# Two blocks of a diffusion transformer in one kernel: tiles moved by 128 and 96 bytes, and pieces of the modulation rows loaded one or two chunks earlier

## The chip, the core and the metric

The kernel runs on one core of one Trainium2 chip. The metric is the device time of one execution in microseconds (us); smaller is better. The profile adds a trace of one execution: every instruction's start and duration on each engine (PE is TensorE, DVE is VectorE, ACT is ScalarE, POOL is GpSimd, SP is SyncE, which issues the DMAs).

## The reference, cut to what matters

Two "macaron" transformer blocks follow each other on 256 tokens of width 1024, each with two layers, all in float32. A layer is feed-forward, mixer, feed-forward; that makes twelve phases. Each phase is preceded by a norm whose scale and shift, and followed by a residual whose gate, come from a modulation row:

```
mod = (silu(c) @ ada_w[l] + ada_b[l])            # 9 rows of 1024 for a layer
pre(h, j) = rmsnorm(h, norm_g[l, j]) * (1 + mod[:, j, 1]) + mod[:, j, 0]
x = x + 0.5 * (1 + mod[:, 0, 2]) * swiglu(pre(x, 0), ffn_wi[l, 0], ffn_wo[l, 0])
x = x + (1 + mod[:, 1, 2]) * mixer(pre(x, 1))
x = x + 0.5 * (1 + mod[:, 2, 2]) * swiglu(pre(x, 2), ffn_wi[l, 1], ffn_wo[l, 1])

swiglu(h, wi, wo): gt, up = split(h @ wi); (silu(gt) * up) @ wo      # wi 1024 x 5632, wo 2816 x 1024
```

The mixers are an HGRN2 recurrence ("hgrn") and a differential attention ("diff") in the first block, and twice a sparse attention beside a spatial gate ("nsa") in the second, whose modulation and residual differ slightly in form. All weights, some 530 MB, are read once from memory.

## The kernel before, in words

**Weights.** They come in chunks of 512 rows by 512 columns. `load_chunk` takes a chunk in two halves; each half is one DMA into a tile `raw` and is then split in two: ACT rounds it to the short float32 form (`hi`, L197), and DVE takes the rest (`lo`, L198). The pool `split` holds eight `hi` and eight `lo` tiles, four chunks in all; loading runs ahead of use as far as these go.

**Matmuls.** A product of float32 numbers is made of three matmuls on split operands. In the token-major form (`mm3`, L454 to L456) the activations are the stationary operand, which TensorE loads before the matmul (128 columns, LDWEIGHTS), and 512 columns of the weights stream past it: hi by hi, lo by hi, hi by lo. The activations are `hT` (the normed input, transposed, for the first product of a phase), `aT` (the gated hidden values of a feed-forward, for its second product), and for the mixers' last products `y`, `k`, `q`, `oT`. In the feature-major form (`feature_block`, L550 and L552) the weights are the stationary operand and the activations stream: one matmul of `hi` with 512 columns (both parts of `hT` for 256 tokens) and one of `lo` with 256 columns. Most of the first product of a feed-forward is feature-major: chunks 4 to 21 of its 34 (8 to 21 in the first phase), two chunks to a block, 70 blocks of 32 such pairs in the whole kernel. The mixer hgrn has its own feature-major form with three matmuls of 256 columns (L611 to L613).

**Modulation rows.** Each row of 1024 values is made of four pieces. A piece (`ada`) loads two tiles `araw` of 128 rows of `ada_w`; DVE multiplies each by a column of silu(c) and adds it up (`accumulate`, L264). When the eighth is in, `row_sum` adds over the partitions with TensorE: ACT and DVE split one half of the accumulator (`acch` L276, `accl` L277, one buffer each), TensorE sums it with a matrix of ones (L281, L282), and the result becomes shift, scale or gate; then the second half goes the same way.

**The order of the work.** `build` writes one queue with all chunks and, between them, the pieces for the gate of this phase and the scale and shift of the next. `ADA_SPAN` says for each kind of phase how many chunks at its start (skip) and at its end (tail) get no piece; the pieces are spread evenly over the chunks between. Loads are issued by SyncE in the queue's order; the number of pieces loaded sets when the sums of DVE and TensorE's row sums stand in their engines' orders. Every engine works through its instructions in order.

**Where tiles lie.** Pools are laid one behind another in each partition's memory: const, keep (with `hT`), raw, split (`hi`, then `lo`), tmp (with `acch`, `accl`), and then one pool per phase ("act" with `aT`, or the mixer's).

Of the kernel before, what the change touches and what calls it, by code (L numbers as in the profile page):

```python
# [10 lines left out]
F32R = mybir.dt.float32r  # L11
# [7 lines left out]
P = 128  # L19
D = 1024  # L20
# [11 lines left out]
W_LATER = 15  # L32
FFN_TR, QK_TR, HN_TR, MRG_TR, NSA_TR = 2, 1, 3, 2, 2
W5, XS, SG, RING, GF = 4, 4, 2, 5, 5
WARM = 60

ADA_SPAN = {"first": (11, 6), "ffn": (5, 5), "hgrn": (2, 11), "diff": (3, 6), "nsa": (2, 6), "last": (3, 10)}

NSA_PLAN = [(1, "setup"), (2, "spatial_load"), (6, "pick"), (6, "load_w1", 0, 0), (7, "load_w1", 1, 0),
            (8, "load_w1", 0, 1), (8, "load_w1", 1, 1), (10, "hidden", 0), (12, "hidden", 1), (15, "hidden_tr"), (16, "compressed"),  # L40
# [24 lines left out]
class Chunk:  # L65


    def __init__(self, src, nk, heads=0):
        self.src = src
        self.nk = nk  # L70
        self.heads = heads
        self.parts = None

    def hi(self, k):
        return self.parts[k // 2][0][:, k % 2, :]
# [5 lines left out]
class Net:  # L81
    def __init__(self, ctx, tc, A):
        self.tc = tc
        self.nc = tc.nc
        self.A = A
        self.const = ctx.enter_context(tc.tile_pool(name="const", bufs=1))
        self.keep = ctx.enter_context(tc.tile_pool(name="keep", bufs=1))
        self.rawp = ctx.enter_context(tc.tile_pool(name="raw", bufs=RAWS))
        self.split = ctx.enter_context(tc.tile_pool(name="split", bufs=HALVES))
        self.tmp = ctx.enter_context(tc.tile_pool(name="tmp", bufs=2))  # L90
        self.psm = ctx.enter_context(tc.tile_pool(name="psm", bufs=6, space=PSUM))
        self.pst = ctx.enter_context(tc.tile_pool(name="pst", bufs=2, space=PSUM))
        self.queue = []
        self.next_item = 0
        self.chunks = []
        self.used = [0, 0]
        self.loaded = 0
        self.pend = []
        self.row_stages = []
        self.araws = []  # L100
        self.gates = {}
        self.phase = None
        self.now = 0
        self.setup()
# [75 lines left out]
    def load_chunk(self, it):  # L180
        nc = self.nc
        it.parts = []
        for h in range((it.nk + 1) // 2):
            n = min(2, it.nk - 2 * h)
            w = it.src[-1][1]
            raw = self.raw()
            for c0, c1, src in it.src:
                if it.heads:
                    for g in range(2):
                        r0 = g * 256 + h * P  # L190
                        nc.sync.dma_start(raw[g * 64:(g + 1) * 64], src[r0:r0 + P].rearrange("(i d) n -> d i n", d=64))
                else:
                    nc.sync.dma_start(raw[:, :n, c0:c1], src[h * 256:h * 256 + n * P].rearrange("(k p) n -> p k n", p=P))
            hi = self.split.tile([P, 2, 512], F32R, tag="hi", name="hi")
            lo = self.split.tile([P, 2, 512], F32R, tag="lo", name="lo")
            r = raw[:, :n, :w]
            nc.scalar.activation(hi[:, :n, :w], r, AF.Copy)  # L197
            nc.vector.tensor_sub(lo[:, :n, :w], r, hi[:, :n, :w].bitcast(F32))  # L198
            it.parts.append((hi, lo))
# [110 lines left out]
    def warm(self):  # L310

        ps = self.bank()
        with self.later(1000):
            for _ in range(WARM):
                self.nc.tensor.matmul(ps.rearrange("p (a b) -> p a b", a=4), lhsT=self.ones,
# [1098 lines left out]
def phases(A, which=None):  # L1414
    out = []
    for b in range(2):
        s = "_2" if b else ""
        wi, wo = (A["ffn_wi"], A["ffn_wo"]) if b == 0 else (A["ffn_w_in_2"], A["ffn_w_out_2"])
        for l in range(2):
            out.append((b, l, 0, ("ffn", wi[l, 0], wo[l, 0])))  # L1420
            out.append((b, l, 1, (("hgrn", "diff")[l] if b == 0 else "nsa", l)))
            out.append((b, l, 2, ("ffn", wi[l, 1], wo[l, 1])))
    return out if which is None else [out[i] for i in which]


def build(ctx, tc, A, which=None):
    net = Net(ctx, tc, A)
    nc = tc.nc
    ph = phases(A, which)
    starts = []  # L1430
    net.next_phase = ph[0][:3]

    def diff_prep():
        net.diff_prep(A["b_qk_g"][0], A["b_lam"][0], A["b_subln"][0], 0.8 - 0.6 * math.exp(-0.3))

    def second_half():
        for kind in (1, 0):
            net.ada_first(kind, 1)
        for T in range(2):
            net.scaled(T, 1)  # L1440
            net.pre(T, (1,))
    for i, (b, l, j, spec) in enumerate(ph):
        ada = net.ada_pieces(b, l, j, 2)
        if i + 1 < len(ph):
            b2, l2, j2, _ = ph[i + 1]
            ada += net.ada_pieces(b2, l2, j2, 1) + net.ada_pieces(b2, l2, j2, 0)
        if spec[0] == "ffn":
            cs = net.ffn_chunks(spec[1], spec[2], i == 0)
        elif spec[0] == "hgrn":
            cs = net.hgrn_chunks(A["a_w_in"][0], A["a_w_out"][0])  # L1450
        elif spec[0] == "diff":
            cs = net.diff_chunks(A["b_w_in"][0], A["b_w_out"][0])
        else:
            cs = net.nsa_chunks(A["mix_w_in_2"][l], A["proj_a_2"][l], A["proj_b_2"][l], A["w_out_2"][l])
        starts.append(len(net.chunks))
        done = 0
        for n, spec_ in enumerate(cs):
            if i == 0 and n == 3:
                net.queue.append(("f", second_half))
            if i + 1 < len(ph) and ph[i + 1][3][0] == "diff" and n == len(cs) // 2:  # L1460
                net.queue.append(("f", diff_prep))
            net.add_w(*spec_)
            skip, tail = ADA_SPAN["first" if i == 0 else spec[0] if i + 1 < len(ph) else "last"]
            want = max(0, n + 1 - skip) * len(ada) // (len(cs) - skip - tail)
            while done < min(want, len(ada)):
                net.add_ada(ada[done])
                done += 1
    net.warm()
    net.ada_first(1, 0)
    for T in range(2):  # L1470
        nc.sync.dma_start(net.x[:, T, :], A["x"][0, T * P:(T + 1) * P, :])
        for h in range(2):
            net.norm_half(T, h)
    net.ada_first(0, 0)
    for T in range(2):
        net.scaled(T, 0)
        net.pre(T, (0,))
    net.ahead()
    net.condition("c_2")
    for i, (b, l, j, spec) in enumerate(ph):  # L1480
        last = i + 1 == len(ph)
        net.phase = b, l, j
        net.next_phase = None if last else ph[i + 1][:3]

        def after(T):
            if not last:
                net.pre(T)
            else:
                for h in range(2):
                    o, rstd = net.xs.pop((T, h)), net.ss[T][:, 3:4]  # L1490
                    if h == 0:
                        nc.scalar.activation(o, o, AF.Copy, scale=rstd)
                    else:
                        nc.vector.tensor_scalar(o, o, rstd, None, op0=OP.mult)
                    nc.sync.dma_start(A["out"][0, T * P:(T + 1) * P, h * 512:(h + 1) * 512], o)
        if last:
            nc.sync.dma_start(net.S, A["final_g_2"][None, :].to_broadcast([P, D]))
            net.rows[1] = None
        if spec[0] == "ffn":
            net.ffn(starts[i], after, i == 0)  # L1500
        elif spec[0] == "hgrn":
            net.hgrn(starts[i], A["a_onorm"][0], after)
        elif spec[0] == "diff":
            net.diff(starts[i], after)
        else:
            net.nsa(starts[i], l, after)
# [22 lines left out]
```

## Time and profile before

| | us |
|---|---|
| median of 3 runs | 2231.85 (2231.0 to 2233.54) |
| the profiled execution's own time | 2231.27 |
| its span, first to last instruction | 2229.5 |
| TensorE (matmuls) busy | 2188.1 (98%) |
| VectorE busy | 1787.6 (80%) |
| ScalarE busy | 1233.3 (55%) |
| mean granted TensorE clock | 0.998 |

A busy TensorE is not one at its peak: a matmul's recorded duration overlaps that of the next. What one costs in a dense stretch is read from the starts: the time from one start to the next. All durations below are of the profiled execution.

### The profile page before, as it was taken

What the parts mean: (1) busy time and instruction counts of PE and PEld (TensorE: products, weight loads), DVE (VectorE), ACT (ScalarE), POOL (GpSimd) and SP (SyncE); (2) the same over time, 40 slices, a digit from 0 to 9 for tenths busy, and PEclk for the clock granted to TensorE, in tenths of its full rate; (3) what the DMA queues carried; (4) which work ended last, traced back from release to release, by engine and by line L of the source; (5) the groups of instructions that cost most, each with busy time, mean ns of one, the idle gap of its engine ahead of it and who ended that gap; (6) DMA issues with size and microseconds to landing.
All of it is one profiled execution on the core that took longest, in us unless ns stands there. A gap on an engine that the chain in (4) does not pass through costs nothing. (4 is left out here: it accounts for less than half of the span.)

```text
span 2229.5 us, 33181 instructions
## 1 busy us (share of the span) xinstructions
PE 2188.1 (98%) x12152; PEld 1808.4 (81%) x12152; DVE 1787.6 (80%) x2481; ACT 1233.3 (55%) x2184; POOL 118.3 (5%) x164
## 2 busy tenths in 40 slices
PE   9999999999999989999999999999999999999998
PEld 6888887888888767888888787788878887777886
DVE  7888898787878789878868788887877878887664
ACT  3554645564565577564565446456446644655653
POOL 1000101000000131000000000000000001000000
PEclk9999999999999999999999999999999999999999
DMA  9888865777857766867767786676777778845553
GB/s 299 303 300 292 297 218 191 265 243 261 276 185 270 255 227 224 277 216 268 262 221 242 257 291 202 223 253 199 264 258 255 263 241 268 266 153 185 187 172 108
DMA packets 264788, 537.19 MB, mean 241 GB/s; under 512 B 22083, under 2 KB 52619, under 8 KB 264625
## 3 DMA queue, kind: packets, MB, share of 16 engines
q1 hardware_dynamic: 264184, 534.67, 72.1%
q8 instruction: 95, 1.56, 0.3%
q14 instruction: 69, 0.56, 0.1%
q10 hardware_dynamic: 440, 0.40, 0.1%
HBM read 533.95 MB, written 1.05 MB: 240 GB/s over the span
## 5 line engine op out<-in xcount | busy, mean ns | idle before, releaser
L198 DVE TENSOR_TENSOR lo<-raw,hi 128x1024 fp32r<-128x1024 f32 (+1 forms) x704 | 846.8, 1215 | 253.9 <-ACT hi L197 250.1
L197 ACT ACTIVATE hi<-raw 128x1024 fp32r<-128x1024 f32 (+1 forms) x704 | 732.7, 1055 | 524.1 <-PE mm L456 303.0
L550 PE MATMUL mm<-hT,hi 128*128 128x512 f32 x2240 | 793.6, 399 | 0.0
L552 PE MATMUL mm<-hT,lo 128*128 128x256 f32 x2240 | 629.5, 281 | 0.0
L550 PEld LDWEIGHTS mm<-hT,hi 128*128 128x128 f32 x2240 | 421.5, 188 | 103.9
L552 PEld LDWEIGHTS mm<-hT,lo 128*128 128x128 f32 x2240 | 423.8, 189 | 1.0
L454 PE MATMUL mm<-hi,hT 128*128 128x512 f32 (+1 forms) x832 | 331.0, 398 | 1.3 <-ACT hT L384 1.0
L456 PE MATMUL mm<-hi,hT 128*128 128x512 f32 (+1 forms) x832 | 324.8, 391 | 0.9 <-DVE hT L386 0.9
L455 PE MATMUL mm<-lo,hT 128*128 128x512 f32 (+1 forms) x832 | 323.3, 389 | 0.0
L456 PE MATMUL mm<-hi,aT 128*128 128x512 f32 x704 | 278.4, 395 | 0.0
L454 PE MATMUL mm<-hi,aT 128*128 128x512 f32 x704 | 278.2, 395 | 0.0
L455 PE MATMUL mm<-lo,aT 128*128 128x512 f32 x704 | 277.6, 394 | 0.0
L454 PEld LDWEIGHTS mm<-hi,hT 128*128 128x128 f32 x832 | 156.5, 188 | 40.3 <-issue 8.0
L264 DVE SCALAR_TENSOR_TENSOR acc<-araw,c_2s,acc 128x1024 f32<-128x1024 f32 x144 | 184.1, 1278 | 2.8 <-DMA araw<-ada_w 1.9
L456 PEld LDWEIGHTS mm<-hi,hT 128*128 128x128 f32 x832 | 156.5, 188 | 35.0 <-DVE hT L386 2.1
L455 PEld LDWEIGHTS mm<-lo,hT 128*128 128x128 f32 x832 | 156.6, 188 | 29.6 <-issue 0.7
L264 DVE SCALAR_TENSOR_TENSOR acc<-araw,cs,acc 128x1024 f32<-128x1024 f32 x128 | 163.5, 1278 | 10.6 <-DMA araw<-ada_w 9.9
L455 PEld LDWEIGHTS mm<-lo,aT 128*128 128x128 f32 x704 | 132.6, 188 | 30.4
L456 PEld LDWEIGHTS mm<-hi,aT 128*128 128x128 f32 x704 | 132.5, 188 | 30.4
L454 PEld LDWEIGHTS mm<-hi,aT 128*128 128x128 f32 x704 | 132.6, 188 | 30.3
L535 ACT ACTIVATE aT<-uf 128x256 fp32r<-128x256 f32 x140 | 58.2, 416 | 87.0 <-DVE uf L533 87.0
L248 POOL MEMSET acc<- 128x1024 f32 x34 | 32.5, 957 | 1240.2 <-DVE accl L277 713.2
(287 smaller groups left out, 2164.5 us busy)
## 6 DMA issues: line engine op xcount, KB each, us to landing
araw<-ada_w SPq DMA_DIRECT2D x272, 512.0 KB
raw<-ffn_wi SPq DMA_DIRECT2D x160, 512.0 KB
raw<-ffn_w_in SPq DMA_DIRECT2D x160, 512.0 KB
raw<-ffn_wo SPq DMA_DIRECT2D x88, 512.0 KB
raw<-ffn_w_out SPq DMA_DIRECT2D x88, 512.0 KB
raw<-mix_w_in SPq DMA_DIRECT2D x64, 512.0 KB
raw<-a_w_in SPq DMA_DIRECT2D x32, 512.0 KB
raw<-b_w_in SPq DMA_DIRECT2D x24, 512.0 KB
```

Source lines behind the costliest of these rows:

```text
L197: nc.scalar.activation(hi[:, :n, :w], r, AF.Copy)
L198: nc.vector.tensor_sub(lo[:, :n, :w], r, hi[:, :n, :w].bitcast(F32))
L248: nc.gpsimd.memset(st["acc"], 0.0)
L264: self.nc.vector.scalar_tensor_tensor(acc, raw, self.cs[b][:, k:k + 1], acc, op0=OP.mult, op1=OP.add)
L454: nc.tensor.matmul(ps, lhsT=h, rhs=hi, start=start and i == 0, stop=False)
L455: nc.tensor.matmul(ps, lhsT=h, rhs=lo, start=False, stop=False)
L456: nc.tensor.matmul(ps, lhsT=l, rhs=hi, start=False, stop=stop and i == c.nk - 1)
L535: nc.scalar.activation(hi, u, AF.Copy)
L550: nc.tensor.matmul(ps[f], lhsT=c.hi(k)[:, fs], rhs=x, start=kh == 0 and k == 0, stop=False, skip_group_check=True)
L552: nc.tensor.matmul(ps[f][:, 0:256], lhsT=c.lo(k)[:, fs], rhs=x[:, 0:256], start=False, stop=kh == 1 and k == 3, skip_group_check=True)
```

## The change: where tiles lie, and when pieces are loaded

First, the tiles of `split` grow from 1024 to 1088 float32 values (4352 bytes), and `hi` and `lo` are a window of 1024 values in them. For the feature-major chunks of the feed-forwards the window begins 24 values (96 bytes) into the tile, for all others at its start. Second, a tile of 32 values (128 bytes) that nobody uses is put at the head of the pool tmp; all that lies behind it, the pools of the phases too, moves by these 128 bytes. Third, in `ADA_SPAN` four kinds of phase have skip smaller and tail larger by one or two, so their pieces stand one or two chunks earlier in the queue.

Where the tiles stand in the two built programs (bytes from the start of a partition):

| tile | before | after | modulo 256, before | modulo 256, after |
|---|---|---|---|---|
| hT | 13,696 | 13,696 | 128 | 128 |
| hi, number k of 8 | 75,136 + 4096 k | 75,136 + 4352 k | 128 | 128; feature-major 224 |
| lo, number k of 8 | 107,904 + 4096 k | 109,952 + 4352 k | 128 | 128; feature-major 224 |
| acch, accl | 159,232, 161,280 | 163,456, 165,504 | 0 | 128 |
| aT, its two parts | 165,376, 187,904 | 169,600, 192,128 | 0 | 128 |
| k0, q0 (hgrn), oT0 (diff), y00 (nsa) | 173,568, 181,760, 189,952, 209,152 | 177,792, 185,984, 194,176, 213,376 | 0 | 128 |

Modulo 512 the tiles `hi` and `lo` before are all at 384; after, they are by turns at 384 and 128 (480 and 224 where shifted), `hT` stays at 384, and `aT` moves from 0 to 128. Inside a tile all operands begin at multiples of 512 bytes.

```
+FM_SHIFT = 24
-ADA_SPAN = {"first": (11, 6), "ffn": (5, 5), "hgrn": (2, 11), "diff": (3, 6), "nsa": (2, 6), "last": (3, 10)}
+ADA_SPAN = {"first": (10, 7), "ffn": (3, 7), "hgrn": (2, 11), "diff": (2, 7), "nsa": (1, 7), "last": (3, 10)}
...
+        self.feature_major = False                                 # Chunk.__init__
...
+        self.t(self.tmp, [P, 32], tag="pad", bufs=1)               # Net.__init__
...
-            hi = self.split.tile([P, 2, 512], F32R, tag="hi", name="hi")
-            lo = self.split.tile([P, 2, 512], F32R, tag="lo", name="lo")
+            s = FM_SHIFT if it.feature_major else 0
+            hi, lo = (self.split.tile([P, D + 64], F32R, tag=n, name=n)[:, s:s + D].rearrange("p (a b) -> p a b", a=2)
+                      for n in ("hi", "lo"))
...
-            net.add_w(*spec_)
+            c = net.add_w(*spec_)
+            net.chunks[c].feature_major = spec[0] == "ffn" and (8 if i == 0 else 4) <= n < 22
```

The numbers of matmuls, splits, sums and DMAs stay as they are; the new `ADA_SPAN` moves sums and row sums in the engines' orders. Lines of the kernel after are four or five higher than those before (L198 is L202, L264 is L268, L276 is L280, L277 is L281). Three places follow.

ScalarE in the first feed-forward, around the split of the second half of the first gate row (`acch`; `gate` is the first half's evacuation, `gf` and `uf` are the gated features, `hi` a weight split). Before:

```order
L197 ACTIVATE hi<-raw 128x1024
L529 ACTIVATE gf<-gf 128x256
L519 ACTIVATE gf<-mm 128x256
L291 ACTIVATE gate<-tr 128x512
L197 ACTIVATE hi<-raw 128x1024
L529 ACTIVATE gf<-gf 128x256
L276 ACTIVATE acch<-acc 128x512
```

And after:

```order
L539 ACTIVATE aT_366<-uf 128x256 x2
L201 ACTIVATE hi<-raw 128x1024 x2
L295 ACTIVATE gate<-tr 128x512
L280 ACTIVATE acch<-acc 128x512
L523 ACTIVATE gf<-mm 128x256 x2
```

The row's evacuation and split now stand ahead of the block's group of `gf`, where before they stood behind most of it.

VectorE at the same place (`lo` is the second part of a weight split, `acc<-araw` a sum of a modulation row, `accl` the second part of the row's split). Before:

```order
L264 SCALAR_TENSOR_TENSOR acc<-araw,cs,acc 128x1024
L198 TENSOR_TENSOR lo<-raw,hi 128x1024
L520 TENSOR_TENSOR gf<-gf,mm 128x256
L198 TENSOR_TENSOR lo<-raw,hi 128x1024
L520 TENSOR_TENSOR gf<-gf,mm 128x256
L264 SCALAR_TENSOR_TENSOR acc<-araw,cs,acc 128x1024
L520 TENSOR_TENSOR gf<-gf,mm 128x256
L264 SCALAR_TENSOR_TENSOR acc<-araw,cs,acc 128x1024
L520 TENSOR_TENSOR gf<-gf,mm 128x256
L198 TENSOR_TENSOR lo<-raw,hi 128x1024 x2
L277 TENSOR_TENSOR accl<-acc,acch 128x512
```

And after:

```order
L268 SCALAR_TENSOR_TENSOR acc<-araw,cs,acc 128x1024
L202 TENSOR_TENSOR lo<-raw,hi 128x1024 x2
L524 TENSOR_TENSOR gf<-gf,mm 128x256
L281 TENSOR_TENSOR accl<-acc,acch 128x512
L524 TENSOR_TENSOR gf<-gf,mm 128x256
L268 SCALAR_TENSOR_TENSOR acc<-araw,cs,acc 128x1024
```

The split of the row moved ahead of two sums, two weight splits and three `gf`; TensorE's row sum, which waits for it, moved earlier by 32 matmuls of the block.

VectorE in the mixer diff, in the first softmax (`ast` are its maxima and sums, `w<-e,ast` the finished weights, `rb`, `ra` a rotary product beside it). Before:

```order
L975 SCALAR_TENSOR_TENSOR ast<-ast,qs 128x4
L277 TENSOR_TENSOR accl<-acc,acch 128x512
L974 TENSOR_REDUCE ast<-mm 128x4
L975 SCALAR_TENSOR_TENSOR ast<-ast,qs 128x4
L979 RECIPROCAL ast<-ast 128x4
L264 SCALAR_TENSOR_TENSOR acc<-araw,cs,acc 128x1024
L979 RECIPROCAL ast<-ast 128x4
L264 SCALAR_TENSOR_TENSOR acc<-araw,cs,acc 128x1024
L981 TENSOR_SCALAR ast<-ast,lm 128x4
L198 TENSOR_TENSOR lo<-raw,hi 128x1024
L986 SCALAR_TENSOR_TENSOR w_7929<-e,ast 128x128 x4
```

And after:

```order
L979 SCALAR_TENSOR_TENSOR ast<-ast,qs 128x4
L978 TENSOR_REDUCE ast<-mm 128x4
L925 TENSOR_TENSOR w_7892<-ra,rb 128x8x16
L979 SCALAR_TENSOR_TENSOR ast<-ast,qs 128x4
L268 SCALAR_TENSOR_TENSOR acc<-araw,cs,acc 128x1024 x2
L983 RECIPROCAL ast<-ast 128x4
L268 SCALAR_TENSOR_TENSOR acc<-araw,cs,acc 128x1024 x2
L983 RECIPROCAL ast<-ast 128x4
L268 SCALAR_TENSOR_TENSOR acc<-araw,cs,acc 128x1024
L985 TENSOR_SCALAR ast<-ast,lm 128x4
L202 TENSOR_TENSOR lo<-raw,hi 128x1024
L990 SCALAR_TENSOR_TENSOR w_7943<-e,ast 128x128 x4
```

Five sums stand inside this softmax now, where two stood; they come from the later part of the phase, which has three fewer.

## Rows read from the trace of the kernel before

**Rows 1.** The page, part 1: busy us (share of the span) xinstructions.

```profile
PE 2188.1 (98%) x12152; PEld 1808.4 (81%) x12152; DVE 1787.6 (80%) x2481; ACT 1233.3 (55%) x2184; POOL 118.3 (5%) x164
```

**Rows 2.** Stretches: from:to us, length, busy us (xinstructions) of each engine, clock, DMA.

```profile
52.00:2160.00 2108.00, 2078.06 (x11714) 1726.22 (x11715) 1720.51 (x2394) 1193.88 (x2129) 108.52 (x142) 1.00 0.73 244
1097.00:1104.00 7.00, 7.00 (x33) 5.79 (x32) 6.92 (x8) 3.69 (x5) 0.00 (x0) 1.00 0.92 307
1223.00:1265.00 42.00, 42.00 (x183) 34.03 (x182) 32.18 (x32) 17.45 (x21) 0.74 (x2) 1.00 0.84 286
2070.00:2150.00 80.00, 80.00 (x455) 69.31 (x454) 55.46 (x87) 48.97 (x86) 0.00 (x0) 1.00 0.59 185
153.50:164.40 10.90, 10.90 (x64) 9.59 (x64) 10.68 (x17) 7.09 (x13) 0.00 (x0) 1.00 0.86 309
147.20:150.60 3.40, 3.26 (x10) 2.79 (x11) 2.36 (x3) 1.67 (x3) 0.96 (x1) 0.50 0.88 276
833.30:836.70 3.40, 3.40 (x13) 2.95 (x13) 3.40 (x6) 1.60 (x4) 0.00 (x0) 0.50 0.50 166
```

**Rows 3.** Timeline of PE, ends of four stretches: start us, us, instruction.

```profile
153.34 0.39 PE L550 MATMUL mm<-hT,hi 128*128 128x512 f32 x1
...
164.08 0.39 PE L550 MATMUL mm<-hT,hi 128*128 128x512 f32 x1
...
1096.67 0.39 PE L456 MATMUL mm<-hi,hT 128*128 128x512 f32 x1
...
1103.92 0.39 PE L455 MATMUL mm<-lo,hT 128*128 128x512 f32 x1
...
1222.65 0.39 PE L454 MATMUL mm<-hi,aT 128*128 128x512 f32 x1
...
1264.94 0.39 PE L456 MATMUL mm<-hi,aT 128*128 128x512 f32 x1
...
2069.86 0.40 PE L550 MATMUL mm<-hT,hi 128*128 128x512 f32 x1
...
2149.71 0.40 PE L550 MATMUL mm<-hT,hi 128*128 128x512 f32 x1
```

**Rows 4.** Groups by line: line engine op names xcount | busy us, mean ns | idle before.

```profile
L550 PE MATMUL mm<-hT,hi 128*128 128x512 f32 x2240 | 793.6, 399 | 0.0
L456 PE MATMUL mm<-hi,hT 128*128 128x512 f32 x800 | 315.3, 395 | 0.9 <-DVE hT L386 0.9
L454 PE MATMUL mm<-hi,aT 128*128 128x512 f32 x704 | 278.2, 395 | 0.0
L456 PE MATMUL mm<-hi,y 128*128 128x512 f32 x64 | 25.2, 394 | 0.0
```

**Rows 5.** Timeline of PE at the first row sum's second half; in brackets, idle before.

```profile
143.66 0.28 PE L552 MATMUL mm<-hT,lo 128*128 128x256 f32 x1
145.92 0.50 PE L281 MATMUL tr<-acch,ones 128*128 128x512 f32 x1 [1.98 <-ACT acch L276]
147.34 0.80 PE L282 MATMUL tr<-accl,ones 128*128 128x512 f32 x1 [0.93 <-DVE accl L277]
```

**Rows 6.** Timeline of ACT and DVE there.

```profile
133.27 1.99 ACT L197 ACTIVATE hi<-raw 128x1024 fp32r<-128x1024 f32 x2
136.53 1.28 DVE L264 SCALAR_TENSOR_TENSOR acc<-araw,cs,acc 128x1024 f32<-128x1024 f32 x1 [1.29 <-DMA araw<-ada_w]
144.33 2.35 DVE L198 TENSOR_TENSOR lo<-raw,hi 128x1024 fp32r<-128x1024 f32 x2
```

**Rows 7.** Waits of PE: who waited for whom, us in total, times, longest us.

```profile
PE tr L397 <- DVE xs L378: 7.5, 15, 0.8
PE tr L397 <- DVE w L921: 5.2, 3, 2.1
PE tr L397 <- DVE w L986: 1.0, 1, 1.0
```

**Rows 8.** Timeline of DVE in the mixer diff's first softmax.

```profile
804.35 0.18 DVE L979 RECIPROCAL ast<-ast 128x4 f32<-128x4 f32 x1 [1.87 <-ACT e L977]
```

## The prediction

> **What bounds the kernel.** I read the page's busy times first. TensorE is busy for 98% of the span, VectorE for 80%, ScalarE for 55% [rows 1], and the stretches say where the missing 2% lies: between 52 and 2160 us TensorE stands still for 2108.00 - 2078.06 = 30 us only [rows 2]. The rest of the span is matmul behind matmul, so the time is the number of matmuls times the distance from one start to the next, plus these 30 us. The recorded duration (395 ns) is no price, since it overlaps the next one; the reader must go to the timeline, take the first and the last start of a dense stretch, and divide by the number of matmuls between them, which the stretches give. I did it for four stretches, all at full clock (1.00):
>
> - token-major with `hT` as stationary operand: 33 matmuls of 512 columns in [rows 2], from 1096.67 to 1103.92, 7.25 us over 32 steps, 226.6 ns a step [rows 3];
> - token-major with `aT`: 183 matmuls of the same shape, from 1222.65 to 1264.94, 42.29 over 182, 232.4 ns;
> - feature-major: the 455 matmuls are 227 pairs and one more; from 2069.86 to 2149.71 are 226 pairs of 768 columns, 353.3 ns a pair;
> - feature-major again, right after a disturbance: 64 matmuls, 153.34 to 164.08, 31 pairs, 346.5 ns.
>
> The first two differ in nothing that the program says but where the operands lie. `hi`, `lo` and `hT` all stand at 128 modulo 256 bytes; `aT` stands at 0. Stationary and moving operand a multiple of 256 bytes (here even of 512) apart: the quick step. 128 bytes off that: 5.8 ns slower, every time. The last two are one instruction sequence on tiles that lie the same, and run at two steady paces; the quick one is rare, as the mean duration of L550 over all 2240 (399 ns) is that of the slow stretch and not the 0.39 of the other [rows 3, 4].
>
> **The change part by part.** *The 128 bytes before tmp.* They put `aT` at 128 modulo 256, which is where `hi` and `lo` stand unshifted. L454 to L456 with `aT` are 3 x 704 = 2112 matmuls [rows 4]. If they take the step of `hT`: 2112 x 5.8 ns = 12.2 us. After each interruption the pace has to be found again, and `hT` loses more there than `aT` does (its runs are short); I take 10 us. The `y` of nsa (3 x 64), and k, q and oT of hgrn and diff (3 x 32) move to 128 as well; their mean duration of 394 is like `aT`'s [rows 4], and 288 x 5.8 would be 1.7 us; their runs are short, so I take 1. Together 11 us, bounds 0 (the place decides nothing) and 13.9. A loss here has a case of its own below.
>
> *The 96 bytes under the feature-major weights.* Here stationary (`hi`, `lo`) and moving (`hT`) are a multiple of 512 bytes apart before, and the slow pace rules. After, they are 96 bytes off. No stretch before has 96 bytes, so I bound it. Above: if any distance costs what 128 bytes cost token-major, 5.8 ns for each of two matmuls, a pair takes 365 and 2240 pairs lose 26 us. Below: a pair at the token-major quick step by columns, 226.6 x 768 / 512 = 340 ns, gains 2240 x 13.3 = 30 us. The nearest row is the quick pace of the same instructions, 346.5: 6.8 ns a pair. One of 70 blocks and part of another have it already, so about 2180 pairs gain 14.8 us; I take 14.5, keeping both ends.
>
> *The larger split tiles* (4352 bytes) keep `hi`, `lo` at 128 modulo 256, and so should leave the 800 x 3 matmuls on `hT` [rows 4] where they are: 0, if 256 is the period (see the rivals if it is 512).
>
> *The pieces earlier.* No instruction is added; each sum (1.28 us on VectorE, [rows 6]), its two DMAs on SyncE and its row sum on TensorE move together. SyncE's weight loads between old and new place come up to two DMAs later, and VectorE's splits behind them; TensorE waits for no weight split in a long wait [rows 7], so I cost that at 0; if the cover were gone, it would be the two DMAs' sums, 2.6 us on VectorE. What can move are two known stalls.
> First feed-forward: TensorE ends at 143.66 + its step, then stands 2.0 us for `acch` and 0.9 for `accl` [rows 5], and after that its clock is at half (0.50, 1.2 GHz) for 3.4 us [rows 2], 1.7 us lost: 4.6 in all. Now `acch` is ahead of the `gf` group on ScalarE and `accl` ahead of two sums and two weight splits on VectorE, but TensorE asks 32 matmuls (5.65 us) earlier too, at about 138.1. By the old rows: ScalarE is at its two `hi` until 135.3, evacuates and splits the row by about 136.5; VectorE waits for `araw` until 136.53, sums until 137.8, splits two weights (2.35) and runs one `gf` first, so `accl` is there at about 141 [rows 6]. The wait would be 2.9 us, as before: the stall moves and stays. Value 0, bounds -4.6 and +1.5.
> Mixer diff: three more sums stand in the first softmax, 3.8 us, of which VectorE's old idle time there hides 1.87 [rows 8]; TensorE's wait for `w` L986, 1.0 us [rows 7], may become 2.9. The later rotary product, for which it waits 2.1 us [rows 7] with another 3.4 us at half clock behind it [rows 2], has three sums fewer ahead of it: -2.1 - 1.7. Value -1, bounds -3.8 and +1.9.
> The waits for `xs` (15 of up to 0.8 us, [rows 7]) hang on the last row and the norm at each phase's end; the third row's sums stay there, 0.
>
> Sum: -11 - 14.5 - 1 = -26.5 us on the execution's own 2231.3, which lies 0.6 under the median of the runs: 2205 us for the median.
>
> By the Trainium skill's page "SBUF — State Buffer" (section "Who interferes with whom") TensorE never waits on any other engine for SBUF, and only VectorE and GpSimd share ports; "TensorE: Matmul & The Clock Gate" (Part 2, step by step) adds that TensorE's two read ports are independent, so loading the next weights takes nothing from the running matmul. By that rule the place of a tile could not matter, and the sum would be that of the moved pieces alone. The steps of 226.6 and 232.4 ns speak against it, without proving that the place is what parts them.
>
> **The rivals.**
> *Near is what counts* (slower). In the trace the token-major step is best at distance 0 and worse at 128 bytes. If TensorE pays by the distance within 256 bytes, then moving the feature-major weights from 0 to 96 is a step in the wrong direction, and 2240 pairs pay up to 11.6 ns: -11 - 1 + 26 gives 2245; it decides from a pair of about 359 on, where it eats the other gains (12 / 2240 = 5.4 ns over 353.3). For it: the only two token-major distances seen. Against: feature-major runs at its slow pace at distance 0, so nearness alone does not give the quick one.
> *Feature-major keeps its pace.* Two paces on the same addresses show that what came before decides the pace, not only the place; then the 96 bytes do nothing: 2231.9 - 12 = 2220. For it: the quick stretch came right behind the half-clock stretch.
> *The period is 512 bytes, not 256.* All good stretches seen are multiples of 512. With tiles 4352 bytes apart, every second `hi` and `lo` is then 256 off `hT` and `aT`. If that costs as 128 do, half of 2400 matmuls on `hT` lose 5.8 ns (+7), `aT` and the others gain half (-5.5), feature-major half (-7): about 2225. Nothing before stands 256 apart, so neither for nor against.
> *The place does nothing.* `aT` is slower because it lies far up in the partition, or for its neighbours in time. Then only the pieces count: 2231 (2227 to 2235). It is also what the skill's rule would give. For it: no tile changes its place in this trace. Against: `y`, k, q and oT, also at 0 modulo 256, read like `aT` in phases quite unlike.
> *Feature-major goes under its quick pace*, to some 340 a pair: 2190.
>
> **How the numbers follow.** The forecast 0.48 (its own range 2197 to 2213, from the bounds of the two stalls and a restart loss of 0 to 4 us); feature-major unchanged 0.17; period 512, 0.10; nearness 0.12; no effect of place 0.08; under the quick pace 0.05. Faster or slower counts from 0.2% (4.5 us), about what a measurement here can tell. Faster is under 2227.4: the forecast, the lower pace, feature-major unchanged and the period of 512, together 0.80. Slower is over 2236.3: nearness, 0.12. Same: no effect of place, 0.08. The range goes from 2194 to 2231: it leaves out the pace of 340, nearness, and a little of the rest.
>
> **What would show it.** The four stretches, measured again: `aT` at about 227 a step (right) or 232 (the place is not it); a feature-major pair at 346 to 347, in nearly all 70 blocks, or at 353 or above 359; `hT` still at 226.6, and not every second chunk slower. In the waits, `acch` or `accl` of the first row at 2 to 3 us and a half-clock stretch behind; `w` L990 up by one or two us and the later wait for `w` gone. The prediction is wrong if the two paces do not follow the places, most of all if the feature-major pair is above 353.

## The result: 2205.8 us, 1.1% less, and the profile after

The changed kernel takes 2205.83 us (median of 4 runs, 2204.56 to 2207.33) against 2231.43 for the kernel before (4 runs beside it, 2230.53 to 2233.54): a ratio of 0.9887, 95% interval 0.9873 to 0.9900. The forecast was 2205. The span of the profiled execution falls from 2229.5 to 2202.8 us.

In the page, part 1 (busy us, share of the span, instructions), the same 12152 matmuls are busy for 28.6 us less than in [rows 1], while the other engines hardly move:

```profile
PE 2159.5 (98%) x12152; PEld 1803.0 (82%) x12152; DVE 1791.2 (81%) x2481; ACT 1232.7 (56%) x2185; POOL 117.4 (5%) x164
```

So the time went out of the matmuls themselves. To see out of which, I repeat the reading of [rows 2, 3]: stretches without any other instruction on TensorE (from:to, length, busy and instructions of PE, PEld, DVE, ACT, POOL, then clock, DMA share, GB/s), for `hT`, for `aT` and feature-major; the last row is a stretch of half clock.

```profile
1079.10:1088.60 9.50, 9.50 (x44) 7.86 (x43) 9.39 (x10) 5.34 (x6) 0.00 (x0) 1.00 0.88 293
1200.50:1240.00 39.50, 39.50 (x176) 32.72 (x175) 28.25 (x27) 15.62 (x18) 1.32 (x2) 1.00 0.81 274
2051.00:2127.00 76.00, 76.00 (x440) 66.86 (x440) 54.95 (x87) 47.36 (x83) 0.00 (x0) 1.00 0.62 189
290.10:293.50 3.40, 3.40 (x19) 3.40 (x18) 3.40 (x6) 0.22 (x1) 0.00 (x0) 0.50 0.85 263
```

The first and the last start of the three, from the timeline of PE (start us, us, instruction):

```profile
1078.77 0.39 PE L458 MATMUL mm<-hi,hT 128*128 128x512 f32 x1
...
1088.52 0.39 PE L459 MATMUL mm<-lo,hT 128*128 128x512 f32 x1
...
1200.26 0.39 PE L460 MATMUL mm<-hi,aT 128*128 128x512 f32 x1
...
1239.93 0.39 PE L458 MATMUL mm<-hi,aT 128*128 128x512 f32 x1
...
2050.82 0.39 PE L554 MATMUL mm<-hT,hi 128*128 128x512 f32 x1
...
2126.74 0.39 PE L554 MATMUL mm<-hT,hi 128*128 128x512 f32 x1
```

`hT`: 9.75 us over 43 steps, 226.7 ns, as before (226.6). `aT`: 39.67 over 175, 226.7 instead of 232.4. Feature-major: 440 matmuls are 220 pairs, 75.92 over 219, 346.7 ns instead of 353.3. The settled step of `aT` is now that of `hT`, and feature-major runs everywhere at the pace that it had before in a few short stretches alone: of the stretches of 16 pairs or more, all 36 settle (their first steps left out) at 346.6 to 346.8 ns a pair.

The groups by line (xcount | busy us, mean ns | idle before) say the same of whole kernels and are quicker to read: against [rows 4], L554 falls from 399 to 392 ns and `aT` from 395 to 390, `y` by 4, and `hT` hardly moves. They show the direction; the size must come from the starts.

```profile
L554 PE MATMUL mm<-hT,hi 128*128 128x512 f32 x2240 | 779.1, 392 | 0.0
L460 PE MATMUL mm<-hi,hT 128*128 128x512 f32 x800 | 314.6, 394 | 0.5 <-DVE hT L390 0.5
L458 PE MATMUL mm<-hi,aT 128*128 128x512 f32 x704 | 274.7, 390 | 0.0
L460 PE MATMUL mm<-hi,y 128*128 128x512 f32 x64 | 25.0, 390 | 0.0
```

Summing the steps from start to start over both whole traces gives the account of the 26.7 us of span: feature-major 794.5 to 777.5 us (-17.0, of which 2.1 is the old stall of [rows 5], which stood behind one of these matmuls, and 1.2 the pairs that then ran at half clock, so -13.7 by pace), `aT` 497.6 to 487.0 (-10.6), `y` 46.1 to 45.4 (-0.7), everything else +1.6, as the waits shifted.

The stall at the first row sum, from the timeline of PE after (in brackets idle before and its releaser):

```profile
137.73 0.39 PE L285 MATMUL tr<-acch,ones 128*128 128x512 f32 x1
139.28 0.51 PE L286 MATMUL tr<-accl,ones 128*128 128x512 f32 x1 [1.16 <-DVE accl L281]
```

In place of 1.98 and 0.93 us in [rows 5] TensorE waits 1.16 us, and no half clock follows. The waits of PE (us in total, times, longest) that answer [rows 7]:

```profile
PE tr L401 <- DVE xs L382: 8.4, 16, 0.8
...
PE tr L401 <- DVE w L925: 4.6, 3, 1.7
...
PE tr L401 <- DVE w L990: 1.2, 1, 1.2
```

The two half-clock stretches of [rows 2], at 147.2 and 833.3, are gone; one of the same length stands at 290.1, in the hgrn mixer.

### The profile page after: what moved, and what is told of

The parts are those of the page before. It is cut to its first block, busy times and chain, and to the rows that moved or that the text cites. A ratio compares the mean times of both kernels' runs of the same rounds, so it can differ in the third digit from the quotient of the medians.

```text
span 2202.8 us, 33165 instructions
## 1 busy us (share of the span) xinstructions
PE 2159.5 (98%) x12152; PEld 1803.0 (82%) x12152; DVE 1791.2 (81%) x2481; ACT 1232.7 (56%) x2185; POOL 117.4 (5%) x164
## 5 line engine op out<-in xcount | busy, mean ns | idle before, releaser
L202 DVE TENSOR_TENSOR lo<-raw,hi 128x1024 fp32r<-128x1024 f32 (+1 forms) x704 | 847.1, 1216 | 241.9 <-ACT hi L201 233.6
L554 PE MATMUL mm<-hT,hi 128*128 128x512 f32 x2240 | 779.1, 392 | 0.0
L554 PEld LDWEIGHTS mm<-hT,hi 128*128 128x128 f32 x2240 | 420.5, 188 | 92.6
L460 PE MATMUL mm<-hi,aT 128*128 128x512 f32 x704 | 274.8, 390 | 0.0
L458 PE MATMUL mm<-hi,aT 128*128 128x512 f32 x704 | 274.7, 390 | 0.0
L268 DVE SCALAR_TENSOR_TENSOR acc<-araw,c_2s,acc 128x1024 f32<-128x1024 f32 x144 | 184.5, 1281 | 1.7
L268 DVE SCALAR_TENSOR_TENSOR acc<-araw,cs,acc 128x1024 f32<-128x1024 f32 x128 | 164.0, 1282 | 12.5 <-DMA araw<-ada_w 11.6
```

Of the source, the lines that this page charges most:

```text
L268: self.nc.vector.scalar_tensor_tensor(acc, raw, self.cs[b][:, k:k + 1], acc, op0=OP.mult, op1=OP.add)
L458: nc.tensor.matmul(ps, lhsT=h, rhs=hi, start=start and i == 0, stop=False)
L460: nc.tensor.matmul(ps, lhsT=l, rhs=hi, start=False, stop=stop and i == c.nk - 1)
L554: nc.tensor.matmul(ps[f], lhsT=c.hi(k)[:, fs], rhs=x, start=kh == 0 and k == 0, stop=False, skip_group_check=True)
```

## The experiments

**One part of the change at a time.** Three kernels: the pad and the larger split tiles without a shift (`FM_SHIFT = 0`), the shift without the pad, and the pieces' places alone.

```
e1   + self.t(self.tmp, [P, 32], tag="pad", bufs=1);  tiles [P, D + 64], FM_SHIFT = 0;  ADA_SPAN of before
e2   tiles [P, D + 64], FM_SHIFT = 24, no pad;  ADA_SPAN of before
e3   the kernel before with the new ADA_SPAN
```

> The change without the 96 bytes and without the moved pieces: split tiles of 4352 bytes and the phases' tiles 128 bytes further. Place theory (TensorE's step depends on how far stationary and moving operand lie apart, modulo 256 bytes): aT's step goes from 232.4 to about 227 ns, the feature-major pair stays at 353; 2111 x 5.3 + 1 = 12 us faster, 2219 to 2220 us. Rival 'pieces' (the gain came from the sums placed earlier): no change, 2231. Rival 'both at once' (the pace of one form depends on the other's): feature-major moves as well.

> Only the 96 bytes under the feature-major weights (with the wider split tiles, a multiple of 256 for all behind them); aT stays at 0 modulo 256 and the pieces stay. Place theory: the pair goes from 353 to 346.8 ns, aT stays at 232.4; 2180 x 6.2 = 13.5 us faster, about 2218. Rival 'pieces': 2231. Rival 'nearness': slower, 2245.

> Only the pieces one or two chunks earlier; all tiles as before. Forecast of the prediction: about -1 us, 2230 (bounds 2223 to 2235). Place theory: aT's step 232.4 and the feature-major pair 353 as before. Rival 'pieces': 2210 or less.

Measured against the kernel before: tiles 2218.00 us, 0.9951 (0.9935 to 0.9966); shift 2217.78, 0.9951 (0.9938 to 0.9964); places 2228.56, 0.9994 (0.9985 to 1.0003), no difference that can be told. The product is 0.9897, against 0.9887 for the whole. The groups of the kernel with the tiles alone:

```profile
L554 PE MATMUL mm<-hT,hi 128*128 128x512 f32 x2240 | 793.2, 399 | 0.0
...
L458 PE MATMUL mm<-hi,aT 128*128 128x512 f32 x704 | 275.0, 391 | 0.0
```

and of the one with the shift alone:

```profile
L553 PE MATMUL mm<-hT,hi 128*128 128x512 f32 x2240 | 778.8, 392 | 0.0
...
L457 PE MATMUL mm<-hi,aT 128*128 128x512 f32 x704 | 278.5, 396 | 0.0
```

And the steps, from the first and last starts of one stretch each, `aT` with the tiles alone and feature-major with the shift alone:

```profile
1224.97 0.39 PE L458 MATMUL mm<-hi,aT 128*128 128x512 f32 x1
...
1254.89 0.39 PE L458 MATMUL mm<-hi,aT 128*128 128x512 f32 x1
...
2055.14 0.39 PE L553 MATMUL mm<-hT,hi 128*128 128x512 f32 x1
...
2135.22 0.39 PE L553 MATMUL mm<-hT,hi 128*128 128x512 f32 x1
```

29.92 us over 132 steps are 226.7 ns, 80.08 over 231 pairs 346.7. The other form stays slow in each: the pair at 353.3 with the tiles alone, `aT` at 232.4 (first and last phase) to 233.3 with the shift alone. Each edit moves the form that it was put under: two independent gains. Both kernels have the larger tiles, so these alone move neither.

**All tiles by 128 bytes.** If the place in the partition were what counts, moving everything would move the steps; if the distance, nothing would happen.

```
  self.const = ctx.enter_context(tc.tile_pool(name="const", bufs=1))
+ self.t(self.const, [P, 32], tag="pad", bufs=1)
```

> The kernel before with all its tiles 128 bytes further, so that hT, hi and lo stand at 0 modulo 256 and aT at 128: distances as before, places changed over. Place theory by distance: hT stays at 226.6 to 228, aT stays at 232.4, time 2231. Rival 'place by itself' (128 modulo 256 is a good place for the stationary operand, 0 a bad one): hT slows to 232, aT quickens to 227; 2360 x 4 - 2111 x 5.3 = about -2 us. Rival 'level' (aT is slow for lying far up or for its neighbours in time): both as before, and e1 shows no gain.

One run, 2231.20 us, and the groups are those of [rows 4]:

```profile
L551 PE MATMUL mm<-hT,hi 128*128 128x512 f32 x2240 | 794.1, 399 | 0.0
...
L455 PE MATMUL mm<-hi,aT 128*128 128x512 f32 x704 | 278.3, 395 | 0.0
```

From the timeline of PE, 29.98 us over 129 steps of `aT`, 232.4 ns:

```profile
1225.13 0.40 PE L455 MATMUL mm<-hi,aT 128*128 128x512 f32 x1
...
1255.11 0.39 PE L455 MATMUL mm<-hi,aT 128*128 128x512 f32 x1
```

`aT` now stands at 128 modulo 256, where the changed kernel has it, and is as slow as before. The distance between stationary and moving operand is what the gain hangs on, not the place.

**Sweeps.** The eight feed-forward phases are nearly the same work, and in the changed kernel all eight settle at the same two steps, so one run can try eight distances. I gave each phase its own shift, first in steps of 32 bytes, then finer.

```
- s = FM_SHIFT if it.feature_major else 0
+ s = it.shift        # (FM_SHIFT if feature-major else TOK_SHIFT)[feed-forward phase]
e5   FM_SHIFT = [0, 8, 16, 24, 32, 40, 48, 56];  TOK_SHIFT = [32, 40, 48, 56, 0, 8, 16, 24]
e6   FM_SHIFT = [1, 2, 4, 6, 12, 20, 28, 60];    TOK_SHIFT = [2, 4, 6, 12, 20, 28, 36, 1]
```

> The changed kernel with one more table: each of the eight feed-forward phases has a place of its own. Feature-major weights are shifted by 0, 32, 64, 96, 128, 160, 192 and 224 bytes in phases 1 to 8, and the token-major weights of the same phases by 128, 160, 192, 224, 0, 32, 64 and 96 bytes against hT and aT. Theory S (one slow band in each form): the feature-major pair takes 353 ns at 0, something between at 32 and 224, and 346.7 at 64 to 192; a token-major matmul takes 232.4 at 128, something between at 96 and 160, and 227 at 192, 224, 0, 32 and 64; the whole about 2209 us. Rival Q (one quick band in each form, everything else slow): the pair takes 346.7 only at 64 to 128 and 353 in the other five phases, a token-major matmul 227 only at 224, 0 and 32 and 232.4 elsewhere; the whole about 2219 us. Rival B (there is a place better than those of the change): some phase shows a pair under 340 ns or a token-major matmul under 222 ns.

> As the kernel with eight places, with finer steps: feature-major weights shifted by 4, 8, 16, 24, 48, 80, 112 and 240 bytes in the eight feed-forward phases, token-major ones by 8, 16, 24, 48, 80, 112, 144 and 4 bytes. Theory G (places count by grains of 32 bytes or more): the feature-major pair takes 353 ns at 4 to 24 bytes, as at 0, and 346.7 at 80 and 112; a token-major matmul 227 at 4 to 24. Rival F (single words count): already 4 or 8 bytes bring the pair under 350 ns. Rival H (the pace rises evenly with the distance): the pair falls in steps, about 0.07 ns a byte, from 353 at 4 to 347 at 80. The whole about 2210 to 2216 us.

One run each, 2225.13 and 2224.10 us: both slower than any theory gave. (The added table moves the line numbers by one.) The reading is always that of the first and last start in one long uninterrupted stretch of the phase. From the timeline of PE in the coarse sweep, two phases feature-major (64 and 224 bytes) and `aT` at distance 0:

```profile
652.41 0.39 PE L555 MATMUL mm<-hT,hi 128*128 128x512 f32 x1
...
691.63 0.40 PE L555 MATMUL mm<-hT,hi 128*128 128x512 f32 x1
...
1225.62 0.39 PE L460 MATMUL mm<-lo,aT 128*128 128x512 f32 x1
...
1259.84 0.39 PE L461 MATMUL mm<-hi,aT 128*128 128x512 f32 x1
...
2069.71 0.39 PE L555 MATMUL mm<-hT,hi 128*128 128x512 f32 x1
...
2152.91 0.39 PE L555 MATMUL mm<-hT,hi 128*128 128x512 f32 x1
```

39.22 us over 111 pairs are 353.3 ns, 34.22 over 151 steps 226.6, 83.20 over 240 pairs 346.7. In the fine sweep, feature-major at 16 and at 112 bytes (38.47 and 39.22 us over 111 pairs, 346.6 and 353.3):

```profile
647.50 0.39 PE L555 MATMUL mm<-hT,hi 128*128 128x512 f32 x1
...
685.97 0.39 PE L555 MATMUL mm<-hT,hi 128*128 128x512 f32 x1
...
1725.59 0.39 PE L555 MATMUL mm<-hT,hi 128*128 128x512 f32 x1
...
1764.81 0.39 PE L555 MATMUL mm<-hT,hi 128*128 128x512 f32 x1
```

All sixteen distances, worked out so (bytes by which the weights stand ahead of `hT` or `aT`, modulo 256):

| feature-major, ns a pair | bytes |
|---|---|
| 346.6 to 346.8 | 8, 16, 24, 48, 96, 224, 240 |
| 350.0 to 351.0 | 4, 128, 160 |
| 353.2 to 353.4 | 0, 32, 64, 80, 112, 192 |

| token-major with `aT`, ns a step | bytes |
|---|---|
| 226.6 | 0 |
| 228.9 | 64 |
| 231.1 to 232.2 | 8, 16, 80, 112 |
| 233.3 to 234.3 | 24, 32, 48, 96, 128, 144, 160, 192, 224 |
| 237.2 | 4 |

A phase has up to five feature-major stretches, and the upper table holds one of them. At 16, 24, 48, 96, 224 and 240 bytes all are quick, at 32, 64, 80 and 112 all slow, at 128 and 160 all between. At four distances they differ on tiles that lie the same: at 0 bytes 353.3 in the long ones and 346.6 in two of 16 pairs; at 192 bytes 353.4 and, in three of 16 pairs, 349; at 4 bytes 350.0 and 353.3; at 8 bytes 346.7 and, in the longest, 348.9. The kernel before shows it already: in each of the phases 2 to 7 one stretch of 16 pairs, behind a row sum and at full clock, ran at 346.7. In phase 2, that stretch and the one behind it (5.20 us over 15 pairs, 346.7; 30.04 over 85, 353.4):

```profile
465.91 0.39 PE L550 MATMUL mm<-hT,hi 128*128 128x512 f32 x1
...
471.11 0.39 PE L550 MATMUL mm<-hT,hi 128*128 128x512 f32 x1
...
475.10 0.40 PE L550 MATMUL mm<-hT,hi 128*128 128x512 f32 x1
...
505.14 0.40 PE L550 MATMUL mm<-hT,hi 128*128 128x512 f32 x1
```

So at some distances something besides the place decides, perhaps what ran before; no run here tests it. What sets the 96 bytes of the change apart from 0 is that every stretch settles at the quick pace.

Of the theories only F, that single words count, is borne out (8 bytes bring the pair to 346.8 to 348.9). There is no band: feature-major is quick at 48 and 96 and slow at 64, 80 and 112, with neither nearness nor grains of 32 bytes in it; rival Q was right that most distances are slow, but of its token-major band (224, 0 and 32) only 0 is quick. That most of the untried distances are slow is why both sweeps took longer than expected. And none of the thirty-two readings lies under the change's own 346.7 and 226.7 by more than the 0.1 ns that such a reading can tell.

**The two halves apart.** In everything so far the tile that a matmul uses and the one loaded beside it, for the next matmul, have the same distance to the stream. Shifting the high and low halves of the weights differently tells them apart.

```
+ for n, s in zip(("hi", "lo"), it.shift)
e8   FM_SHIFT = [(24, 0), (0, 24), (56, 0), (0, 56), (4, 0), (0, 4), (24, 16), (16, 24)]
     TOK_SHIFT = [(0, 32), (32, 0), (0, 16), (16, 0), (0, 8), (8, 0), (0, 48), (48, 0)]
```

> In the kernels before this one the high and the low half of a weight chunk stand at the same place, so the tile of a matmul and the tile that is loaded beside it (the next one's) have the same distance to hT. Here the two halves are shifted apart, with another pair of shifts in each feed-forward phase: feature-major (high, low) = (96, 0), (0, 96), (224, 0), (0, 224), (16, 0), (0, 16), (96, 64), (64, 96) bytes; token-major (0, 128), (128, 0), (0, 64), (64, 0), (0, 32), (32, 0), (0, 192), (192, 0). In a feature-major pair the low half is loaded beside the 512 columns of the high half's matmul. Theory N (the load beside the stream decides, and the longer stream most): (96, 0), (224, 0), (16, 0) and (96, 64) take 351 to 353 ns a pair, as 0 and 64 alone do, (0, 96), (0, 224), (0, 16) and (64, 96) take 347 to 348. Rival O (the distance of a matmul's own tile decides): the other way round. Rival M (each half counts for its matmul): all eight between 349 and 351. Token-major matmuls by all three: the low half moves in one of three, so (0, x) loses a third and (x, 0) two thirds of the 6 ns of x alone, 229 and 231 ns, unless a stream that is thrown out once in three settles on no pace at all (232 to 234 in both).

One run, 2222.16 us. In bytes, (high, low): (96, 0) 346.7; (0, 96) 351.6; (224, 0) 344.5; (0, 224) 353.2; (16, 0) 350.0; (0, 16) 346.8; (96, 64) 347.9; (64, 96) 353.3 ns. By these readings the matmul's own high half would decide at 96 and 224 bytes and the low half that is loaded beside it at 16, which fits none of the three theories. Each is one stretch again, and others of the same phases differ: (96, 0) runs at 350.0 over 64 pairs beside the 346.7 over 128, (0, 16) at 353.4 in two stretches of 16 pairs, (96, 64) at 353.4 in three. So the run gives no order of the halves. Token-major, (0, x) took 228.9 to 233.4 and (x, 0) 228.9 to 234.3, without a third or two thirds of anything in it: (128, 0) is quicker than 128 in both halves (228.9 against 233.4), (64, 0) slower than 64 in both (233.3 against 228.9). What meets what inside TensorE stays open. One phase lies under the pace of the change. Its first and last start, 38.24 us over 111 pairs:

```profile
646.91 0.40 PE L554 MATMUL mm<-hT,hi 128*128 128x512 f32 x1
...
685.15 0.39 PE L554 MATMUL mm<-hT,hi 128*128 128x512 f32 x1
```

**Is that a better place?** More pairs around it in one run; the high half at 224 in all phases, timed; and the changed kernel itself on the same chip.

```
e9    FM_SHIFT = [(56, 8), (56, 4), (56, 16), (56, 32), (56, 48), (60, 0), (52, 0), (56, 60)]
e10   FM_SHIFT = 56;  for n, s in (("hi", s), ("lo", 0))
e11   as changed
```

> The third phase of the kernel with split places (high half at 224 bytes, low half at 0) took 344.7 ns a pair, 2 ns below the 346.7 of the change, though neither 0 nor 224 alone gives less than 346.7. Here the high half stands at 224 in six phases with the low half at 32, 16, 64, 128, 192 and 240, and the pairs (240, 0) and (208, 0) fill the other two. Theory D (the step of the stationary tile from one matmul to the next counts, besides its distance to the stream): (240, 0) and (208, 0) take 343 to 346 too, and some of the six lie under 346. Rival L (346.7 is the floor of a settled stream, and (224, 0) an accident of that phase): none lies under 346.5. Token-major halves (0, 16), (0, 240), (0, 96), (0, 160), (0, 4), (0, 224), (128, 224), (128, 32): none under 226.7 by either, 228 to 234.

> The changed kernel with the high half of feature-major weights at 224 bytes and the low half at 0 in all eight phases. If the 344.7 ns a pair holds in all of them, 2240 x 2.0 = 4.5 us less than the changed kernel, about 2201 us or a ratio to the kernel before of 0.987. Rival: it was that phase alone, the others fall to 346.7 to 351, and the time is 2206 to 2212.

> The changed kernel unaltered, beside the others on one chip: 0.9887 of the kernel before, about 2205 us.

The pairs, in bytes: (224, 32) 348.8, (224, 16) 346.8, (224, 64) 346.8, (224, 128) 348.8, (224, 192) 346.7, (240, 0) 349.9, (208, 0) 346.7, (224, 240) 346.7 ns: none under 346.5, in a run of 2217.84 us, and token-major none under 228.9, as both expected. (These too are one stretch each; (224, 128) ran at 346.7 in another.) With the high half at 224 everywhere: 2201.50 us, 0.9873 (0.9854 to 0.9891); the changed kernel beside it: 2204.13, 0.9879 (0.9861 to 0.9897). Third and last feed-forward phase of the former, from the timeline of PE:

```profile
649.01 0.39 PE L554 MATMUL mm<-hT,hi 128*128 128x512 f32 x1
...
687.25 0.39 PE L554 MATMUL mm<-hT,hi 128*128 128x512 f32 x1
...
2069.81 0.39 PE L554 MATMUL mm<-hT,hi 128*128 128x512 f32 x1
...
2135.68 0.39 PE L554 MATMUL mm<-hT,hi 128*128 128x512 f32 x1
```

344.5 ns over 111 pairs, and 346.7 over 190, on tiles that lie the same. Over the whole phases it is 345.5 in six, 345.9 in the first and 346.6 in the last. The 128 pairs of the third phase that settled at 344.4 in the kernel with split places settle at 346.7 here. So 346.7 is no floor, but the lower pace holds for part of the time only: 2.6 us in the medians where 4.5 were expected, and the intervals overlap. It has the lowest time of all; that it beats the changed kernel is not shown.

**The shifts without the pieces' places**, the changed kernel with the `ADA_SPAN` of before:

> The changed kernel with the old places of the modulation pieces: both shifts and nothing else. If the two shifts add up as they did alone, 0.9951 x 0.9951 = 0.990, about 2208 us, and the pieces' places are worth about 1 us here too. Rival: with quicker matmuls the loads and the modulation rows are later against TensorE, and the pieces' places are worth more than they were on the kernel before (2212 us or more: the long waits for the first feed-forward phase's sums and the half clock after them are back). Rival: the pieces' places cost something in the quicker kernel (2204 or less).

2206.32 us, 0.9897 (0.9878 to 0.9916): the shifts add up as they did alone, and the new places cannot be told from nothing here either. Nor can a single trace tell it: the wait for `accl` in the first feed-forward phase, 1.16 us in the profile after, is no property of the places. In the changed kernel run again TensorE does not wait at all:

```profile
137.71 0.39 PE L285 MATMUL tr<-acch,ones 128*128 128x512 f32 x1
137.93 0.39 PE L286 MATMUL tr<-accl,ones 128*128 128x512 f32 x1
```

and in the kernel with the high half at 224, which has the same pieces at the same places, it waits 1.98 us, and 3.4 us at half clock follow:

```profile
139.84 0.39 PE L285 MATMUL tr<-acch,ones 128*128 128x512 f32 x1
142.21 0.50 PE L286 MATMUL tr<-accl,ones 128*128 128x512 f32 x1 [1.98 <-DVE accl L281]
```

## Why the prediction was right, step by step

*The bound.* Right: the time was matmuls times the step from start to start, at a busy share of 98% before and after.

*The 128 bytes.* Forecast -10 for `aT` and -1 for the rest; measured -10.6, and for the rest -0.7 in `y` and -0.2 in `k` and `q`. The step fell to that of `hT`, as said. That the tiles alone are worth 0.9951 and that moving everything by 128 bytes is worth nothing shows the cause: the distance. What the distance acts on inside TensorE is not shown. The rule drawn in the prediction from the Trainium skill's page "SBUF — State Buffer" (section "Who interferes with whom"), by which the place could not matter, does not hold for these steps: 226.7 against 232.4 ns for one instruction at two distances. That section speaks of engines among themselves, and the step from it to TensorE's own two operands is what fails. The prediction's other sentence, on the two read ports, is about these operands; whether the distance acts there, no run shows.

*The 96 bytes.* Forecast -14.5, measured -13.7 by pace. The size came from the right row, the quick stretch of [rows 3]. But the argument for it was thin: the prediction had no reason why 96 bytes should bring that pace, and the sweeps show that of sixteen distances nine would not have, in the stretches read. It was a choice among the rows, with 0.48 on it, and that it turned out right was in part luck. One reading of the trace was short: not one block and part of another had the quick pace before, but 139 of the 2240 pairs, 43 behind the half clock and six stretches of 16, which makes the gain some 0.5 us smaller than forecast.

*The larger tiles at no cost.* Right: `hT` keeps 226.7, with tiles an odd multiple of 256 bytes apart. The rival of 512 falls; and as 128 and 64 bytes differ from 0 token-major, a period of 128 or 64 would not do.

*The pieces.* Forecast -1; alone 0.9994, which agrees and proves nothing. The step on the first stall, "the stall moves and stays", is not borne out: the wait varies between 0 and 1.98 us among runs with the same places, so a bound was all that could be given, and the 1.75 us (1.98 + 0.93 - 1.16) by which it shrank in the profile after, and the 1.2 us of half clock that went with them, are not shown to be a merit of the change. In the diff mixer the rotary product's long wait and its half clock were to go: in the trace after the half clock is gone, but the wait only fell, from 2.06 to 1.21 us; over all traces the half-clock stretch between 820 and 855 us is in all five with the old places and in two of eight with the new. `w` L990 rose by 0.2 us, not by one or two. What was not foreseen is the half clock at 290 us in hgrn, which ate part of it: it stands, between 288 and 308 us, in five of the eight traces with the new places and in one of the five with the old. TensorE's stop just before it, 2.14 us, was there in the trace before too (2.06), with no half clock behind.

*The rivals.* Nearness falls with both tables. "Feature-major keeps its pace" falls as a forecast, since one shift of tiles brings nearly every pair to 346.7; its premise stands in part: one placement can run at two paces (353.3 and 346.7 at 0 bytes, 344.5 and 346.7 with the halves apart), but that what came before picks the pace is not shown. What it cited for itself, that the quick stretch came right behind the half-clock stretch, is weak: six others came at full clock. "The place does nothing" falls. "Under its quick pace" did not come with the change's places, and came in part with others.

## What to carry to other kernels

Where one matmul form runs in dense stretches, take the step from start to start in each stretch and compare stretches by the distance of their operands modulo 256 bytes; equal instructions at different steps are worth a placement. Do not reason from one distance to the next: try them in one run, a distance for each of several equal phases, and time only what is left. Read every stretch of a phase, since the same tiles can settle at different paces. A pad of 128 bytes and tiles 256 bytes larger added no instruction here and gave 0.5%.

## What the runs showed of the hardware

A token-major matmul of 512 columns had a settled step between 226.6 and 237.2 ns, and a feature-major pair of 768 columns one between 344.5 and 353.4, depending on the distance of the operands to within a few bytes: 4 and 8 bytes apart differ by 5.0 ns (237.2 and 232.2). At some distances the pair has more than one settled pace (353.3 and 346.7 at 0 bytes); at 96 it had one in all traces of the change. At full clock (2.4 GHz) the change's two paces are 544 and 832 cycles, which is 32 cycles for each matmul beyond its columns; that 344.5 ns exist says that these 32 are not fixed. Why some distances settle there and others do not, and what picks the pace where there are two, these runs leave open.
